# Low halves of the weights: a subtraction on VectorE replaced by an accumulating transfer from DRAM

## The chip, the cores and the metric

The kernel runs on one core of one Trainium2 chip. The metric is the device time of one execution in microseconds. Two runs of the kernel before gave 2388.38 and 2389.43 us; their median is 2388.9 us. All inputs and outputs are in DRAM (HBM) at the start and the end.

## The reference

The reference is one inference step of a two-layer trunk for 128 prompt tokens and 512 sample tokens, model width 2048, in float32. The two groups share all weights. Each layer does, for every token:

```python
h = rms_norm(x, norm_g) * (1 + scale) + shift        # scale, shift, gate = silu(cond) @ ada_w + ada_b
p = h @ w_in                                         # 2048 x 6656, all branches in one projection
y = concatenate([branch_1(p) * silu(gate_1), branch_2(p) * silu(gate_2)])
x = x + gate * (y @ w_out)                           # 2048 x 2048
```

Layer 0 has windowed grouped-query attention with a sink and a gated width-3 convolution as its branches. Layer 1 has differential attention (two softmax maps a head) and dense grouped-query attention. Sample tokens also read 256 cached keys and values and use rotary positions. The outputs are the tokens of both groups and the prompt's new keys and values.

Nearly all the arithmetic is in the projections: 640 tokens times 2 x (2048 x 6656 + 2048 x 2048) weights.

## The kernel before

**Numbers in two halves.** TensorE multiplies in a rounded form of float32 (F32R in the code). To keep float32 accuracy, each operand x is split into a high half, x rounded, and a low half, x minus the high half. A product is three matmuls: high by high, activation low by weight high, activation high by weight low.

**Blocks and quarters.** A projection job computes 128 output columns for all 640 tokens; its sum over 2048 input features runs in four quarters of 512 features. A quarter needs one weight block of 512 x 128 numbers (256 KB in DRAM, in rows of 512 bytes), held in SBUF as 128 partitions x 4 x 128. `load_raw` loads it with one transfer on SyncE's queue. `split_w` makes the halves `wh` and `wl` by the helper `split`: ScalarE rounds, VectorE subtracts. `proj_q` then runs 24 matmuls of 128 x 320: four 128-feature pieces, three products, two halves of the tokens (`pa` and `pb`). The tiles `raw`, `wh` and `wl` have four buffers each (`W_BUFS`).

**What runs ahead.** `run_tiles` runs one list of jobs: the input projection of layer 0 (52 jobs), its output projection (16), then the same for layer 1. In steady running it loads a block five quarters ahead of use (`RAW_AHEAD`) and splits it three quarters ahead (`SPLIT_AHEAD`). The first three or five jobs of a list (the leading products) run side by side, quarter by quarter, while the activations `hi` and `lo` of the layer are made. At the very start these share time with the modulation matmuls (`ada_on_pe`, tiles `ada_w`), whose weights are loaded by SyncE in blocks of 512 KB.

**What runs between quarters.** Work that follows a projection (norms, rotary, attention, gates) is cut into steps that are issued between quarters. The rest of the modulation is done on VectorE from 256 KB tiles `adaw` (`ada_on_dve`), some steps per quarter. Softmax exponentials and the rounding of attention operands run on ScalarE, the maxima, scalings and subtractions on VectorE. GpSimd computes a few small powers for the norms (tiles `r`, `rq`, `rn`) and issues the stores: finished branch outputs `y` to a scratch `yd`, the residual `x` to `xd`, the new keys and values, and the outputs. Each engine works through its own queue in order and waits at an instruction until its inputs are there and its buffer is free.

The page's line 208 is the rounding on ScalarE and line 209 the subtraction on VectorE, both in `split`, which is called for weights and for activations alike; the tile's name tells them apart. Lines 240 to 242 are the three products.

Of the kernel before, what the change touches and what calls it, by code (L numbers as in the profile page):

```python
# [15 lines left out]
ALU = mybir.AluOpType  # L16
# [4 lines left out]
P = 128  # L21
# [34 lines left out]
def trunk_kernel(ctx: ExitStack, tc: tile.TileContext, I: dict, O: dict):  # L56
# [26 lines left out]

# [1 line left out]
    ident = const.tile([P, P], F32, name="ident")  # L85
# [17 lines left out]
    for i, n in enumerate(("a_q_norm", "c_q_norm", "d_q_norm")):  # L103
        nc.scalar.dma_start(rows_b[74 + i:75 + i, :], I[n])
    # twice silu(cond) in rows, then features on partitions
    th = pre.tile([32, P], F32, name="th")
# [18 lines left out]

# [1 line left out]
    def ada_done(l, cb, h=0, n=4):  # L127
# [17 lines left out]
    def ada_on_pe(l, cb, pool, h=0, n=4):  # L145
        """The whole block, or half h of it (n of its four 128-column parts)."""
        acc, m, wd = psT(), 8 // n, n * P
        for kt in range(KT):
            if kt % m == 0:
                w = pool.tile([P, m, wd], F32, tag="ada", name="ada_w", bufs=ADA_BUFS)  # L150
                nc.sync.dma_start(w, I["ada_w"][l, kt * P:(kt + m) * P, cb * 512 + h * 256:cb * 512 + h * 256 + wd]
                                  .rearrange("(k p) n -> p k n", p=P))
            g = kt % 4
            PE.matmul(acc[32 * g:32 * g + 32, 0:wd], sT[:, kt, :], w[:, kt % m, :],  # L154
                      start=(kt < 4), stop=(kt >= KT - 4), tile_position=(0, 32 * g))
        sb = pool.tile([P, 512], F32, tag="ada_sb", name="ada_sb", bufs=1)
        A.copy(sb[:, 0:wd], acc[:, 0:wd])
        tr = psT()
        for j in range(n):
            PE.transpose(tr[:, j * P:(j + 1) * P], sb[:, j * P:(j + 1) * P], ident)  # L160
        red = small.tile([P, n, 2], F32, tag="red", name="red", bufs=2)
        V.tensor_reduce(red, tr[:, 0:wd].rearrange("p (b g c) -> p b c g", b=n, g=4)[:, :, 0:2, :], axis=AX.X,
                        op=ALU.add)
        add_bias(l, cb, red, h, n)
        ada_done(l, cb, h, n)
# [39 lines left out]

# [1 line left out]
    def split(hi, lo, x):  # L207
# [9 lines left out]

# [1 line left out]
    def load_raw(w_ap, col, qd, js=(0, 4)):  # L219
        raw = wpool.tile([P, js[1] - js[0], P], F32, tag="raw", name="raw")  # L220
        nc.sync.dma_start(raw, w_ap[(qd * 4 + js[0]) * P:(qd * 4 + js[1]) * P, col:col + P]
                          .rearrange("(k p) n -> p k n", p=P))
        return raw

    def split_w(raw):
        wh = wpool.tile(raw.shape, F32R, tag="wh", name="wh")
        wl = wpool.tile(raw.shape, F32R, tag="wl", name="wl")
        split(wh, wl, raw)
        return wh, wl
# [14 lines left out]
    def new_pp(i):  # L244
        """Two banks for a projection: a pair of them turn about, the third is the scores'."""
        if i == 2:
            t = pS.tile([P, 1024], F32, tag="S", name="Sp")
            return t[:, 0:512], t[:, 512:1024]
        return tuple(pproj.tile([P, 512], F32, tag=f"p{h}{i}", name=f"p{h}") for h in "ab")

    # Work that follows a projection runs in steps between the quarters of later projections.
    prep, attn = [], []
# [20 lines left out]
    def run_tiles(jobs, w_ap, make_h, fill=None, rate=0.0, ahead=None, order=(0, 1, 2, 3), before=None,  # L273
                  last=None, by_half=False, trans=[], grace=0, cut=None):
        if trans:
            lp = tc.tile_pool(name="lead", bufs=1, side="right")
            lead_pool = lp.__enter__()
            sums = {n: lead_pool.tile([P, NT], F32, name=f"sum{n}") for n in trans}
            held = [n for n in range(2 + len(trans)) if n not in trans]
            # a product that is summed on chip between two that stay in PSUM  # L280
            leads = [n for m in range(len(held) + 1) for n in trans[m:m + 1] + held[m:m + 1]]
            leads += trans[len(held) + 1:]
        else:
            leads, held, lp = list(range(min(3, len(jobs)))), [], None
# [4 lines left out]
        for ui, (pos, qd, js) in enumerate(units):  # L289
            parts = {n: split_w(load_raw(w_ap, jobs[n][0], qd, js)) for n in leads[:W_BUFS]}  # L290
            for hv in [HV[:1], HV[1:]] if by_half and pos == 0 else [HV]:
# [4 lines left out]
                for n in leads:  # L296
# [12 lines left out]
                    advance(attn, 1)  # L309
        # quarters of the other projections: loaded RAW_AHEAD and split SPLIT_AHEAD quarters before their use  # L310
        quarters = [(col, qd) for col, _ in jobs[lead:] for qd in range(4)]
# [17 lines left out]
        def settle():  # L329
            """Finish the work that follows the leading products."""  # L330
            while pending:
                n = pending.pop(0)
                drain(prep)
                if before:
                    before(n)
                begin(jobs[n][1], pps[n])
            drain(prep)
# [43 lines left out]
    def to_rows(src, sample):  # L381
        """Tokens on partitions: the sample's four blocks, or the prompt's one."""
        t = psT()
        for i, b in enumerate(range(4) if sample else (4,)):
            PE.transpose(t[:, i * P:(i + 1) * P], src(b), ident)  # L385
        return t if sample else t[:, 0:P]
# [10 lines left out]

# [1 line left out]
    def k_gen(ap, pp, tag, src, gain, new_out):  # L399
# [44 lines left out]

# [1 line left out]
    def q_gen(ap, pp, tag, gain, then=None, wait=True):  # L446
# [22 lines left out]
        for j in range(2):  # L469
            PE.transpose(t[:, j * 96:(j + 1) * 96], sb[:, j * P:(j + 1) * P], ident[0:96, 0:96])  # L470
        # columns: blocks 0, 2, 3 and 1, 3, 4
        u = small.tile([P, 6], F32, tag="ss", name="u")
# [36 lines left out]

# [1 line left out]
    def soft(ap, width, s, n, rsc, nsink=None, sink=None):  # L511
# [17 lines left out]
    def pt_group(ap, pieces):  # L529
        """Up to four 128-wide blocks of P, transposed and split."""  # L530
        t = psT()
        n = len(pieces) * P
        for i, p in enumerate(pieces):
            PE.transpose(t[:, i * P:(i + 1) * P], p, ident)  # L534
        hi = ap.tile([P, 512], F32R, tag="pth", name="pth", bufs=2)
        lo = ap.tile([P, 512], F32R, tag="ptl", name="ptl", bufs=2)
        split(hi[:, 0:n], lo[:, 0:n], t[:, 0:n])
        return hi, lo
# [13 lines left out]

    # the prompt's 128 keys are read with the 128 before them, which the softmax leaves out
    PROMPT_SEGS = [(0, CTX + NS - P, 2 * P)]
    DENSE_SEGS = [(128, 0, 384), (512, 384, 384)]

    def blk_plan(blk, banded):
        """Score segments, masks, the softmax's columns and the key chunks of a query block."""
        if blk == 4:
            return PROMPT_SEGS, (), P, 2 * P, [6]  # L560
        if not banded:
            return DENSE_SEGS, (), 128, 896, [0, 1, 2, 3, 4, 5]
        lo_b, hi_b = max(0, blk - 1), min(3, blk + 1)
        nb = (hi_b - lo_b + 1) * P
        masks = []
        if blk > 0:
            masks.append((mask_lo, 512))
        if blk < 3:
            masks.append((mask_hi, 512 + (blk + 1 - lo_b) * P))
        return ([(256, 0, CTX), (512, CTX + lo_b * P, nb)], masks, 256, 512 + nb,  # L570
                [0, 1] + [2 + b for b in range(lo_b, hi_b + 1)])

    def pair_gen(ap, width, k, banded, emit, done, sinks):
        """Two query heads that share keys and values."""
        v = st["v"]
# [93 lines left out]

    # ======== start: x normalised and transposed, layer 0 modulation ========  # L670
    xT = [sp.tile([P, 4, NT], F32, name=f"xT{g}") for g in range(4)]
# [57 lines left out]

    # ======== layer 0: windowed attention and gated short convolution ========  # L730
    def k_job(tag, src, gain, new_out):
# [13 lines left out]
    def pair_then(width, kk, i, banded, gated):  # L745
        """Attention of heads whose outputs are y[i] and y[i + 1]."""
        def then():
# [88 lines left out]
    for _ in fill0:  # L836
        pass
    # output projection, residual
    x1 = [None] * KT
# [46 lines left out]

    # layer 1 normalisation: half of the tokens while the last product of the other half runs
    def out_last(pp, h):
# [47 lines left out]

    # ======== layer 1: differential attention and dense attention ========
    def odd_start():
# [24 lines left out]
    def diff_gen(ap, h, gt):  # L963
        """Two softmax maps over the same values, the second weighted by -lambda."""
        v = st["v"]
# [166 lines left out]
def _shape_constants():  # L1132
    """Arrays that depend on shapes alone: identity, rotary tables, band edges."""
    t = np.arange(NS)
# [34 lines left out]
```

## Time and profile before

| | |
|---|---|
| median of two runs | 2388.9 us |
| span of the profiled execution (no other time is recorded for it) | 2390.2 us |
| TensorE busy | 2349.4 us, 98% |
| VectorE busy | 1368.3 us, 57% |
| ScalarE busy | 882.6 us, 37% |
| GpSimd busy | 122.9 us, 5% |
| bytes moved by transfers | 298.86 MB, mean 125 GB/s |
| share of the 16 DMA engines, hardware and software queues | 38.1% and 2.7% |

PE is TensorE, ACT is ScalarE, DVE is VectorE, POOL is GpSimd and SP is SyncE; a "q" behind the name is the engine's queue for transfers. The hardware queue carries what SyncE and ScalarE issue, the software queue what GpSimd issues. A group of instructions is shown as line, engine, operation, output and inputs, shape and count, then busy time and mean duration in ns, then the idle time before it and what ended that. Matmuls overlap in the pipeline, so their durations add up to more than the span. "DMA share" is the mean busy share of the 16 DMA engines in a stretch.

### The profile page before, as it was taken

What the parts mean: (1) busy time and instruction counts of PE and PEld (TensorE: products, weight loads), DVE (VectorE), ACT (ScalarE), POOL (GpSimd) and SP (SyncE); (2) the same over time, 40 slices, a digit from 0 to 9 for tenths busy, and PEclk for the clock granted to TensorE, in tenths of its full rate; (3) what the DMA queues carried; (4) which work ended last, traced back from release to release, by engine and by line L of the source; (5) the groups of instructions that cost most, each with busy time, mean ns of one, the idle gap of its engine ahead of it and who ended that gap; (6) DMA issues with size and microseconds to landing.
All of it is one profiled execution on the core that took longest, in us unless ns stands there. A gap on an engine that the chain in (4) does not pass through costs nothing.

```text
span 2390.2 us, 41198 instructions
## 1 busy us (share of the span) xinstructions
PE 2349.4 (98%) x16258; PEld 2252.1 (94%) x16258; DVE 1368.3 (57%) x2711; ACT 882.6 (37%) x1878; POOL 122.9 (5%) x169
## 2 busy tenths in 40 slices
PE   6999999999999999999999999999999999999999
PEld 3579999999999999999999999999999999999999
DVE  4268666765855564666775535454454554576562
ACT  4135342443421223222374434434434444453221
POOL 0001000000000000000000100101000000000000
PEclk9999999999999999999999999999999999999999
DMA  9774325424444445666532221212222212236552
GB/s 330 249 241 132 115 80 157 140 62 150 125 146 126 137 135 158 195 180 191 147 95 65 72 77 54 84 56 83 66 73 59 65 49 80 61 115 213 186 171 79
DMA packets 380128, 298.86 MB, mean 125 GB/s; under 512 B 17842, under 2 KB 321519, under 8 KB 379935
## 3 DMA queue, kind: packets, MB, share of 16 engines
q1 hardware_dynamic: 373104, 273.79, 38.1%
q0 software_dynamic: 6288, 22.22, 2.7%
q8 instruction: 128, 2.10, 0.4%
q14 instruction: 66, 0.53, 0.1%
q10 hardware_dynamic: 542, 0.22, 0.0%
HBM read 273.62 MB, written 22.54 MB: 124 GB/s over the span
## 4 chain that ended last, share of the span: by engine, by line
PE 91%; DVE 3%; DMA 3%; ACT 2%; issue 1%; POOL 0%; SPq 0%; DVEq 0%; ACTq 0%; POOLq 0%
PE pa L240 12%; PE pb L241 12%; PE pb L240 12%; PE pb L242 12%; PE pa L242 12%; PE pa L241 12%; PE T L534 2%; PE T L154 2%; PE S L546 1%; PE S L548 1%; PE S L547 1%; PE T L385 1%; PE T L595 1%; DVE acc L180 1%; DMA ada_w<-in_ada_w 1%
## 5 line engine op out<-in xcount | busy, mean ns | idle before, releaser
L208 ACT ACTIVATE wh<-raw 128x512 fp32r<-128x512 f32 (+1 forms) x549 | 342.9, 627 | 1026.1 <-PE pb L241 895.3
L209 DVE TENSOR_TENSOR wl<-raw,wh 128x512 fp32r<-128x512 f32 (+1 forms) x549 | 374.7, 684 | 534.7 <-ACT wh L208 487.3
L240 PE MATMUL pa<-hi,wh 128*128 128x320 f32 x2112 | 671.9, 318 | 4.7 <-DVE gg L777 1.7
L241 PE MATMUL pa<-lo,wh 128*128 128x320 f32 x2112 | 655.6, 311 | 1.0 <-DVE lo L209 1.0
L242 PE MATMUL pa<-hi,wl 128*128 128x320 f32 x2112 | 654.3, 310 | 0.3 <-DVE wl L209 0.3
L242 PE MATMUL pb<-hi,wl 128*128 128x320 f32 x2112 | 654.2, 310 | 0.0
L240 PE MATMUL pb<-hi,wh 128*128 128x320 f32 x2112 | 653.5, 310 | 0.0
L241 PE MATMUL pb<-lo,wh 128*128 128x320 f32 x2112 | 653.5, 309 | 0.0
L240 PEld LDWEIGHTS pa<-hi,wh 128*128 128x128 f32 x2112 | 397.5, 188 | 28.5 <-issue 20.2
L241 PEld LDWEIGHTS pa<-lo,wh 128*128 128x128 f32 x2112 | 398.1, 189 | 4.9 <-issue 2.9
L241 PEld LDWEIGHTS pb<-lo,wh 128*128 128x128 f32 x2112 | 396.6, 188 | 3.8 <-issue 3.8
L242 PEld LDWEIGHTS pb<-hi,wl 128*128 128x128 f32 x2112 | 396.6, 188 | 3.8 <-issue 3.8
L240 PEld LDWEIGHTS pb<-hi,wh 128*128 128x128 f32 x2112 | 396.5, 188 | 3.3 <-issue 3.3
L242 PEld LDWEIGHTS pa<-hi,wl 128*128 128x128 f32 x2112 | 397.3, 188 | 2.1 <-issue 1.2
L180 DVE SCALAR_TENSOR_TENSOR acc<-adaw,sT,acc 128x512 f32<-128x512 f32 x480 | 336.4, 744 | 27.7 <-DMA adaw<-in_ada_w 27.2
L520 ACT ACTIVATE p<-S,nm,rq 128x768 f32<-128x768 f32 (+3 forms) x120 | 101.2, 844 | 116.8 <-DVE nm L515 80.8
L513 DVE TENSOR_REDUCE nm<-S 128x1 f32<-128x768 f32 (+3 forms) x120 | 91.8, 765 | 23.3 <-PE S L548 22.8
L208 ACT ACTIVATE pth<-T 128x512 fp32r<-128x512 f32 (+1 forms) x132 | 65.7, 533 | 64.6 <-PE T L534 64.5
L209 DVE TENSOR_TENSOR ptl<-T,pth 128x512 fp32r<-128x512 f32 (+1 forms) x132 | 77.3, 608 | 6.2 <-ACT pth L208 4.8
L534 PE MATMUL T<-ident,p 128*128 128x128 f32 x452 | 64.5, 273 | 0.1
L454 ACT COPY qsw<-qx 32x512 f32<-32x512 f32 x96 | 59.3, 618 | 5.6 <-DVE m L430 4.2
L154 PE MATMUL T<-ada_w,sT 128*32 128x512 f32 (+1 forms) x320 | 54.1, 530 | 3.7 <-DMA ada_w<-in_ada_w 3.3
(247 smaller groups left out, 2302.0 us busy)
## 6 DMA issues: line engine op xcount, KB each, us to landing
adaw<-in_ada_w SPq DMA_DIRECT2D x256, 256.0 KB, 3.2
raw<-in_od_w_in SPq DMA_DIRECT2D x208, 256.0 KB, 2.9
raw<-in_ev_w_in SPq DMA_DIRECT2D x203, 256.0 KB, 3.0
ada_w<-in_ada_w SPq DMA_DIRECT2D x64, 512.0 KB, 7.2
raw<-in_ev_w_out SPq DMA_DIRECT2D x64, 256.0 KB, 2.9
raw<-in_od_w_out SPq DMA_DIRECT2D x64, 256.0 KB, 2.9
yd<-y POOLq DMA_DIRECT2D x32, 320.0 KB, 3.0
yin<-yd SPq DMA_DIRECT2D x28, 320.0 KB, 4.1
```

The lines of the kernel that those rows point to most:

```text
L154: PE.matmul(acc[32 * g:32 * g + 32, 0:wd], sT[:, kt, :], w[:, kt % m, :], start=(kt < 4), stop=(kt >= KT - 4), tile_position=(0, 32 * g))
L180: V.scalar_tensor_tensor(out=acc[c], in0=w, scalar=sT[:, kt, c:c + 1], in1=acc[c], op0=ALU.mult, op1=ALU.add)
L208: A.activation(hi, x, AF.Copy)
L209: V.tensor_sub(lo, x, hi)
L240: PE.matmul(ps, wh[:, i, :], hi[:, sl], start=(j == js[0] if alone else (pos == 0 and j == 0)), stop=False)
L241: PE.matmul(ps, wh[:, i, :], lo[:, sl], start=False, stop=False)
L242: PE.matmul(ps, wl[:, i, :], hi[:, sl], start=False, stop=(j == js[1] - 1 if alone else (pos == 3 and j == 3)))
L385: PE.transpose(t[:, i * P:(i + 1) * P], src(b), ident)
L454: A.copy(sw[32 * d:32 * d + 32, :], x[32 * (d ^ 1):32 * (d ^ 1) + 32, 0:NS])
L513: V.tensor_reduce(nm, s, axis=AX.X, op=ALU.max, negate=True)
L520: A.activation(p[:, 0:n], s, AF.Exp, scale=rsc, bias=nm, accum_out=l)
L534: PE.transpose(t[:, i * P:(i + 1) * P], p, ident)
```

## The change

The low half of a weight block is made in another way. ScalarE writes minus the rounded block into `wl`. A transfer issued by GpSimd then reads the same block from DRAM a second time and adds it to what `wl` holds, so that `wl` becomes the block minus its rounded form. ScalarE then writes `wh` as before. VectorE takes no part. `load_raw` returns the DRAM view beside the tile, so that `split_w` can name it. The splitting of activations (`split`) is as before. The lines of comments that the diff also drops are left out here.

```diff
     def load_raw(w_ap, col, qd, js=(0, 4)):
         raw = wpool.tile([P, js[1] - js[0], P], F32, tag="raw", name="raw")
-        nc.sync.dma_start(raw, w_ap[(qd * 4 + js[0]) * P:(qd * 4 + js[1]) * P, col:col + P]
-                          .rearrange("(k p) n -> p k n", p=P))
-        return raw
+        src = w_ap[(qd * 4 + js[0]) * P:(qd * 4 + js[1]) * P, col:col + P].rearrange("(k p) n -> p k n", p=P)
+        nc.sync.dma_start(raw, src)
+        return raw, src
 
     def split_w(raw):
+        raw, src = raw
         wh = wpool.tile(raw.shape, F32R, tag="wh", name="wh")
         wl = wpool.tile(raw.shape, F32R, tag="wl", name="wl")
-        split(wh, wl, raw)
+        A.activation(wl, raw, AF.Copy, scale=-1.0)
+        nc.gpsimd.dma_start(wl, src, accum_op=ALU.add)
+        A.activation(wh, raw, AF.Copy)
         return wh, wl
```

## The prediction

> **What bounds the kernel now.** I read the page's totals first, then the chain that ended last, then its groups.
>
> ```profile
> span 2390.2 us, 41198 instructions
> ...
> PE 2349.4 (98%) x16258; PEld 2252.1 (94%) x16258; DVE 1368.3 (57%) x2711; ACT 882.6 (37%) x1878; POOL 122.9 (5%) x169
> ...
> q1 hardware_dynamic: 373104, 273.79, 38.1%
> q0 software_dynamic: 6288, 22.22, 2.7%
> ...
> PE 91%; DVE 3%; DMA 3%; ACT 2%; issue 1%; POOL 0%; SPq 0%; DVEq 0%; ACTq 0%; POOLq 0%
> ...
> L208 ACT ACTIVATE wh<-raw 128x512 fp32r<-128x512 f32 (+1 forms) x549 | 342.9, 627 | 1026.1 <-PE pb L241 895.3
> L209 DVE TENSOR_TENSOR wl<-raw,wh 128x512 fp32r<-128x512 f32 (+1 forms) x549 | 374.7, 684 | 534.7 <-ACT wh L208 487.3
> ```
>
> TensorE is busy for 98% of the span and makes 91% of the chain. VectorE, which the change relieves, has 57%, and its subtraction (684 ns, 549 times) mostly waits for ScalarE. TensorE idles 2390.2 - 2349.4 = 41 us in all, so no edit that leaves the matmuls alone gains more than that, 1.7%. How far ahead of use is a block made? The timeline of the first output projection shows the third product's matmuls on the low half, and the two halves being made:
>
> ```profile
> 1061.73 0.69 DVE L209 TENSOR_TENSOR wl<-raw,wh 128x512 fp32r<-128x512 f32 x1
> ...
> 1062.27 0.31 PE L242 MATMUL pb<-hi,wl 128*128 128x320 f32 x1
> ...
> 1062.47 0.63 ACT L208 ACTIVATE wh<-raw 128x512 fp32r<-128x512 f32 x1 [2.84 <-PE pb L241]
> ...
> 1065.37 0.68 DVE L209 TENSOR_TENSOR wl<-raw,wh 128x512 fp32r<-128x512 f32 x1
> ...
> 1065.79 0.31 PE L242 MATMUL pb<-hi,wl 128*128 128x320 f32 x1
> ```
>
> From the last matmul of one quarter (1062.27) to that of the next (1065.79) is 3.52 us. ScalarE starts at 1062.47, when a quarter has just released a buffer. There are four buffers, so that one is next read after the other three, 3 x 3.52 = 10.6 us later. Today the low half is ready at 1066.05, 3.8 us after the release. The other resource the change uses is the transfers, so I cut the span into stages; the matmuls of line 242 count the blocks used (eight a block):
>
> ```profile
> core 0: us, PE busy (x) PEld busy (x), PEclk, DMA share, GB/s
> 0.00:60.00 60.00, 1.94 (x6) 1.13 (x6) 0.97 0.95 330
> 60.00:180.00 120.00, 49.77 (x160) 30.02 (x161) 1.00 0.75 245
> 180.00:480.00 300.00, 173.51 (x561) 105.31 (x561) 1.00 0.42 125
> 480.00:900.00 420.00, 264.49 (x855) 160.40 (x855) 1.00 0.42 126
> 900.00:960.00 60.00, 40.48 (x131) 24.65 (x132) 1.00 0.55 169
> 960.00:1140.00 180.00, 116.50 (x376) 70.98 (x376) 0.99 0.63 186
> 1140.00:1320.00 180.00, 104.57 (x338) 63.33 (x337) 1.00 0.34 99
> 1320.00:2100.00 780.00, 422.66 (x1368) 256.74 (x1367) 1.00 0.23 69
> 2100.00:2160.00 60.00, 23.66 (x77) 14.46 (x77) 1.00 0.43 142
> 2160.00:2340.00 180.00, 119.80 (x388) 72.69 (x387) 1.00 0.59 181
> 2340.00:2390.00 50.00, 29.75 (x96) 18.02 (x96) 1.00 0.23 67
> ```
>
> The mean share hides this: the DMA engines are 75% busy in the first products, 63% and 59% in the two output projections, and 23% in the long attention stage.
>
> **The change part by part.**
>
> *Compute engines.* VectorE loses 549 subtractions, 374.7 us. ScalarE gains 549 passes over the same block; priced as its own rounding (627 ns) that is 344 us, and it goes from 37% to 51%. GpSimd gains 549 issues. Its transfers today, and what transfers take to land:
>
> ```profile
> L656 POOL DMA_DIRECT2D yd<-y x32 | 17.9, 561 | 752.2 <-DVE y L779 532.4 <-DVE y L753 125.8 <-DMA adaw<-in_ada_w 43.9
> L1096 POOL DMA_DIRECT2D out_y_sample<-ot x15 | 11.4, 758 | 206.9 <-ACT ot L1095 206.9
> ```
>
> ```profile
> raw<-in_od_w_in SPq DMA_DIRECT2D x208, 256.0 KB, 2.9
> ...
> out_y_sample<-ot POOLq DMA_DIRECT2D x15, 256.0 KB, 3.9
> xb<-in_x_prompt SPq DMA_DIRECT2D x4, 256.0 KB, 6.4
> ```
>
> The nearest issue is out_y_sample: 256 KB, DRAM rows of 512 bytes as in a weight block, 758 ns. 549 x 0.758 = 416 us more on an engine that is busy 5%. No row shows an accumulating issue; I take 0.76 and bound it by 0.56 (yd, longer rows) and by two such issues, 1.5. None of the three engines becomes full.
>
> *Latency of a low half.* After the release: about 0.2 us, ScalarE 0.63, about 0.1, GpSimd 0.76, then the landing. At the plain landing of 3.9 the sum is 5.6 us, against 3.8 now and 10.6 allowed: 5 us of cover are left. That cover is gone when a landing takes more than 10.6 - 1.7 = 8.9 us; the slowest median of a 256 KB transfer, from the start where the share is 0.95, is 6.4. So I cost the latency in steady running at nothing.
>
> *Queues it is put into.* GpSimd's queue is in order, and the added issue waits for ScalarE. Behind it stand the powers of the norms (r, rq, rn) and the stores of y, x and the outputs. The nearest is rn:
>
> ```profile
> DVE on L1009 <- POOL rn L1008: 14.5, 20, 0.8
> ```
>
> An issue ahead of it makes it up to 0.76 us later, 20 times; the next reader on TensorE is a quarter of matmuls (3.52 us) behind, so nothing. The other way round, a store that waits for VectorE holds the next block's issue for some 2 or 3 us, inside the 5 us of cover. On ScalarE exponentials and rounding of attention stand 0.63 us later behind the extra pass, and VectorE's half of the same chain is 0.68 us earlier: nothing. SP issues the same loads; a raw buffer is now free after ScalarE's second pass instead of VectorE's, 0.63 for 0.68: nothing.
>
> *Transfer time.* This is the term that counts. The change adds 549 blocks, 143 MB beside 299. A block by the hardware queue's rate costs all engines 0.381 x 2390.2 / 273.79 x 0.262 = 0.87 us; by the software queue's, 0.027 x 2390.2 / 22.22 x 0.262 = 0.76. The trace has no accumulating transfer. From below it costs one plain software transfer, 0.76. It must also fetch what the block holds in SBUF, so the nearest rows are a load from DRAM (0.87) plus a transfer that reads SBUF (0.76): 1.63, the value I take. From above I set three copies (two reads and a write, each as a load): 2.6.
>
> By stage, at 1.63: 60 to 180 us has 160/8 = 20 blocks, 20 x 1.63 / 120 = 0.27, share 1.02; 900 to 960 has 16.4, share 0.55 + 0.45 = 1.00; 960 to 1140 has 47, 0.63 + 0.43 = 1.06; 2160 to 2340 has 48.5, 0.59 + 0.44 = 1.03. All others stay under 0.85 (480 to 900: 0.42 + 0.42). What exceeds 1 lengthens the stage: 0.02 x 120 + 0.06 x 180 + 0.03 x 180 = 18 us. At 0.76 no stage exceeds 0.88 and the term is 0.
>
> The Trainium skill (Collectives: The Full Stack, Part 3, "The bandwidth ceiling") says that an add in the transfer engines needs two source reads on one ring and so runs at about half a copy's rate, measured at a ratio of 1.93. By that page, as an estimate, a block would cost 1.93 x 0.87 = 1.7 us and the term would be about 27 us in place of 18. No run here shows it yet.
>
> *Start.* Two places are not covered by running ahead.
>
> ```profile
> 40.00:70.00 30.00, 25.32 (x137) 11.46 (x136) 10.47 (x23) 8.19 (x14) 0.00 (x0) 1.00 1.00 349
> 70.00:90.00 20.00, 19.10 (x102) 11.45 (x102) 3.36 (x9) 3.95 (x8) 0.00 (x0) 1.00 0.35 109
> ```
>
> ```profile
> 50.31 1.20 DVE wl L209 x2
> ...
> 124.67 4.28 DMA raw<-in_ev_w_in
> ...
> 129.05 0.64 ACT wh L208
> ...
> 129.74 0.41 PE Sp L240
> ```
>
> From 40 to 70 us the transfers are full; the first four blocks add 4 x 1.63 = 6.5 us there, and the idle transfers from 70 to 90 (0.35) give most of it back: 2 us. At 124.67 the chain itself runs through a raw block to the matmul; its low half would land 0.63 + 0.76 + 3.9 = 5.3 us after it instead of 1.3: 4 us. Against this, subtractions leave the chain ahead of the first product (50.31): -1 us.
>
> Sum: 18 + 2 + 4 - 1 = 23 us; 2390.2 + 23 = 2413. The span stands 1.3 us above the runs' median of 2388.9, and no other time of the profiled execution is recorded, so I predict **2412 us**, +1%. A change of 2% (48 us; faster than 2341 or slower than 2437) is about what a measurement of this kernel can tell from no change.
>
> **The rivals.**
>
> *Hidden.* A block costs a plain copy (0.76). No stage fills; left are the start's few us: 2386 to 2395. For it: the mean share would be 41% + 549 x 0.76 / 2390 = 58%. Against it: the second read.
>
> *Slower: the transfers become the bound.* The place is the first products, the windowed stage and both output projections, the price is the block's transfer time. It decides from about 1.9 us a block, where the surplus of the four stages passes 48 us with the start. At 2.6: 60 to 180, 1.18, 22 us; 180 to 480 (70 blocks), 1.03, 8; 480 to 900 (107), 1.08, 35; 900 to 960, 1.26, 16; 960 to 1140, 1.31, 56; 2160 to 2340, 1.29, 52: 189 us, 2579. Landing time adds to it: once L, the time from release to landed, exceeds 10.6, the quarter becomes (L + 3.52) / 4, so 2 us more is 0.5 us in each of the 110 or so quarters of the output projections: 55 us. For it: three stages are at the brim already at 1.63. Against it: the long attention stage has room at any of these prices (0.23 + 0.57).
>
> *Slower: GpSimd's issue is the bound.* If an accumulating issue takes more than 3.52 us, the projections go at its pace; at 6 us, 549 x 6 = 3290. Nothing in the trace shows an issue over 0.77 us, and nothing shows one of this kind.
>
> *Faster by over 2%.* It would need 48 us where TensorE idles 41. That the subtraction isn't gone is excluded: the built order has none on VectorE, and 549 more passes on ScalarE and transfers on GpSimd.
>
> **How the numbers follow.** Forecast, 2395 to 2437: 0.38. Hidden: 0.12. Transfers the bound, 2437 to about 2600: 0.36. GpSimd's issue or a landing beyond all rows, above 2600: 0.13. Faster: 0.01. So within 2% is 0.50, slower 0.49, faster 0.01. The range reaches from 2388, inside the hidden case, to 2600, the price of 2.6 with a little landing on top; it leaves out the issue's case and the lowest part of the hidden one. The forecast's own range is 2395 to 2437.
>
> **What would show it.** Right: ScalarE near 1227 us and VectorE near 994; the software queue at 37% of the engines (2.7% + 549 x 1.63 / 2390) and the share at or near 1 in the output projections, 0.6 in the attention stage; landing of the added transfers 4 to 7 us; TensorE's waits for them short, and most of them in those full stages. Hidden: software queue near 20%. Wrong: an added issue that lasts microseconds on GpSimd, a landing above 9 us, or TensorE waiting for low halves in the attention stage too.

## The result, and the profile after

The changed kernel takes 2519.74 us (median of 2517.21 and 2522.26) where the kernel before takes 2388.9: a ratio of 1.0545, 95% interval 1.0528 to 1.0563. The profiled execution has a span of 2520.5 us, 130.3 us longer than before's. The page's totals, its queues and the chain that ended last:

```profile
span 2520.5 us, 42146 instructions
...
PE 2391.6 (95%) x16258; PEld 2285.0 (91%) x16258; DVE 1050.4 (42%) x2162; ACT 1153.2 (46%) x2427; POOL 833.7 (33%) x718
...
q0 software_dynamic: 293600, 164.86, 48.7%
q1 hardware_dynamic: 373104, 273.79, 36.2%
...
PE 73%; DMA 12%; issue 8%; DVE 4%; POOL 1%; ACT 1%; SPq 0%; POOLq 0%; ACTq 0%; DVEq 0%
```

VectorE has lost 318 us of work, and no compute engine but TensorE is near full. TensorE runs the same 16258 matmuls, but idles 2520.5 - 2391.6 = 128.9 us (40.8 before) and is busy 42.2 us longer. 88.1 + 42.2 = 130.3: both need a cause. Transfers are now 12% of the chain (3% before). The page's groups, then its DMA issues (last column: median us from issue to landing):

```profile
L245 PE MATMUL pa<-hi,wl 128*128 128x320 f32 x2112 | 667.2, 316 | 60.5 <-DMA wl<-in_ev_w_in 34.0
...
L230 POOL DMA_DIRECT2D wl<-in_ev_w_in x213 | 274.0, 1349 | 597.6 <-ACT wl L229 463.6
...
L180 DVE SCALAR_TENSOR_TENSOR acc<-adaw,sT,acc 128x512 f32<-128x512 f32 x480 | 339.2, 748 | 143.1 <-DMA adaw<-in_ada_w 141.6
L229 ACT ACTIVATE wl<-raw 128x512 fp32r<-128x512 f32 (+1 forms) x549 | 336.0, 615 | 14.8 <-PE pb L245 14.2
...
wl<-in_od_w_in POOLq DMA_DIRECT2D x208, 256.0 KB, 5.3
...
wl<-in_ev_w_in POOLq DMA_DIRECT2D x203, 256.0 KB, 6.0
...
wl<-in_ev_w_out POOLq DMA_DIRECT2D x64, 256.0 KB, 6.5
```

The same two groups before:

```profile
L242 PE MATMUL pa<-hi,wl 128*128 128x320 f32 x2112 | 654.3, 310 | 0.3 <-DVE wl L209 0.3
...
L180 DVE SCALAR_TENSOR_TENSOR acc<-adaw,sT,acc 128x512 f32<-128x512 f32 x480 | 336.4, 744 | 27.7 <-DMA adaw<-in_ada_w 27.2
```

An issue of an added transfer holds GpSimd for 1.3 us, and its landing takes 5.3 to 6.5 us by the medians of the groups. The third product (line 245, line 242 before) now waits 60.5 us where it waited 0.3, and most of that is for the added transfers. VectorE waits 141.6 us for modulation tiles `adaw`, 27.2 before. TensorE's waits, as total us, times and longest:

```profile
PE pa L245 <- DMA wl<-in_ev_w_in: 34.0, 13, 8.2
PE pa L245 <- DMA wl<-in_ev_w_out: 15.4, 5, 5.4
...
PE pa L245 <- DMA wl<-in_od_w_in: 7.7, 5, 3.4
```

**Where the time goes.** The 549 blocks are used in the same order in every kernel here, so the start of each block's third product can be set against the same one of before. The table gives this lag in us at the edges of the stages; a stage's loss is the difference of two neighbours. Here and below the lags are those of the profiled executions.

| third product of | before, at us | lag after |
|---|---|---|
| block 0 | 54.0 | 4.2 |
| block 32 (start is over) | 232.4 | 45.0 |
| block 208 (first output projection begins) | 939.0 | 64.1 |
| block 272 (turn to layer 1) | 1185.3 | 101.8 |
| block 304 | 1326.5 | 117.4 |
| block 480 (last output projection begins) | 2147.7 | 117.5 |
| end | 2390.2 | 130.3 |

So the start loses 45 us, the rest of layer 0's input projection 19, the first output projection 38, the turn to layer 1 16, the long attention stage nothing, the last projection 13. The windows of the same stages (columns after the stretch and its length: busy time of PE, PEld, DVE, ACT and POOL, the granted clock, the DMA share, GB/s):

```profile
60.00:200.00 140.00, 116.35 (x689) 76.50 (x687) 32.29 (x79) 31.73 (x65) 24.00 (x19) 0.91 0.85 225
1003.00:1079.00 76.00, 65.48 (x408) 64.33 (x408) 35.11 (x55) 28.48 (x53) 22.85 (x20) 0.87 1.07 244
1137.00:1280.00 143.00, 125.58 (x816) 122.58 (x814) 67.17 (x116) 44.62 (x86) 42.91 (x38) 0.92 0.99 214
1420.00:2200.00 780.00, 778.20 (x5447) 764.49 (x5447) 291.34 (x649) 417.50 (x914) 270.93 (x237) 1.00 0.70 123
```

At a share of 0.70 nothing is lost. Where TensorE falls behind in these windows, the share is about 1 or the activations and weights are being made at the last moment (the start), and the granted clock is low too: 0.87 to 0.92. Shares above 1 occur, so 1 is no ceiling of this measure.

**The clock.** Two neighbouring windows around one wait of TensorE show why it is also busy for longer:

```profile
1155.29:1162.12 6.83, 4.04 (x15) 4.05 (x16) 0.15 (x1) 0.00 (x0) 1.40 (x2) 0.50 1.30 217
1162.12:1166.00 3.88, 3.88 (x30) 3.88 (x29) 0.00 (x0) 1.79 (x4) 1.24 (x1) 1.00 1.23 253
```

In the first, TensorE idles 2.8 us and runs 15 matmuls in 4.04 us, 0.27 each, at clock 0.50; in the second 30 in 3.88, 0.13 each, at 1.00. Within the span the clock stands at 0.5 for 116.1 us in 20 stretches, before for 6.8 us in 2. In them TensorE is busy for 87.5 us (6.4 before); at full clock the same work would take half, so they explain (87.5 - 6.4) / 2 = 40.5 of the 42.2 us. A shorter wait can do it too:

```profile
1322.60:1326.00 3.40, 1.48 (x10) 1.20 (x9) 3.37 (x7) 3.40 (x8) 0.74 (x1) 0.99 1.14 182
1326.00:1329.40 3.40, 3.40 (x15) 3.40 (x14) 2.10 (x5) 1.63 (x4) 0.54 (x1) 0.50 0.61 105
```

In the first row TensorE idles 1.92 us of the 3.4, and the whole of the second runs at half clock. The Trainium skill (TensorE: Matmul & The Clock Gate, Part 1) says that the clock halves after an idle window of about 3.4 us and recovers after as long a busy one. The stretches here last 3.4, 6.8, 10.2 and once 13.7 us, which fits windows of that length; but the two rows show the halving behind a window that was idle for little more than half of it, and there the measurement decides.

**Two chains.** At the start, the timelines of ScalarE and GpSimd and then the chain that ended last:

```profile
91.24 0.58 ACT L157 COPY ada_sb<-T 128x512 f32<-128x512 f32 x1 [7.66 <-PE T L154]
91.72 0.63 ACT L229 ACTIVATE wl<-raw 128x512 fp32r<-128x512 f32 x1
...
92.64 5.23 POOL L230 DMA_DIRECT2D wl<-in_ev_w_in  x4 [39.17 <-PE T L160]
```

```profile
92.64 9.26 DMA wl<-in_ev_w_in
...
101.95 0.63 PE pa L245
```

ScalarE's queue stands at a modulation copy for 7.66 us; the four blocks behind it are then made in one go, their issues take 5.23 us, and the landing 9.26 us, with TensorE at the end of it. In the first output projection the same happens by another road (VectorE, ScalarE, GpSimd, then the chain):

```profile
1212.47 2.74 DVE L180 SCALAR_TENSOR_TENSOR acc<-adaw,sT,acc 128x512 f32<-128x512 f32 x4 [4.36 <-DMA adaw<-in_ada_w]
1215.12 0.55 DVE L873 SCALAR_TENSOR_TENSOR x<-pa,hgt,o 128x320 f32<-128x320 f32 x1
...
1216.29 0.74 ACT L886 ACTIVATE sq<-x 128x640 f32<-128x640 f32 x1 [10.48 <-DVE x L873]
...
1216.55 0.59 POOL L881 DMA_DIRECT2D xd<-x  x1 [11.93 <-DVE x L873]
1217.13 2.63 POOL L230 DMA_DIRECT2D wl<-in_ev_w_out  x2
```

```profile
1217.13 8.20 DMA wl<-in_ev_w_out
...
1225.37 0.64 PE pa L245
```

A late modulation tile `adaw` holds VectorE, so the residual `x` is late; ScalarE's square and GpSimd's store of `x` wait for it 10.5 and 11.9 us, and the next low halves stand behind both. The traces alone don't tell how much of this is the transfers' bandwidth and how much the lateness of the low half in itself. That is what the runs are for.

### The profile page after: what moved, and what is told of

Same layout as the page of the kernel before. It is cut to its first block, busy times and chain, and to the rows that moved or that the text cites. A ratio compares the mean times of both kernels' runs of the same rounds, so it can differ in the third digit from the quotient of the medians.

```text
span 2520.5 us, 42146 instructions
## 1 busy us (share of the span) xinstructions
PE 2391.6 (95%) x16258; PEld 2285.0 (91%) x16258; DVE 1050.4 (42%) x2162; ACT 1153.2 (46%) x2427; POOL 833.7 (33%) x718
## 3 DMA queue, kind: packets, MB, share of 16 engines
q0 software_dynamic: 293600, 164.86, 48.7%
## 4 chain that ended last, share of the span: by engine, by line
PE 73%; DMA 12%; issue 8%; DVE 4%; POOL 1%; ACT 1%; SPq 0%; POOLq 0%; ACTq 0%; DVEq 0%
PE pa L245 10%; PE pa L243 10%; PE pb L244 10%; PE pb L243 10%; PE pb L245 10%; PE pa L244 10%; DMA adaw<-in_ada_w 4%; DMA wl<-in_ev_w_in 3%; PE T L537 2%; DVE acc L180 2%; DMA ada_w<-in_ada_w 2%; PE S L549 1%; PE S L551 1%; PE S L550 1%; PE T L388 1%
## 5 line engine op out<-in xcount | busy, mean ns | idle before, releaser
L245 PE MATMUL pa<-hi,wl 128*128 128x320 f32 x2112 | 667.2, 316 | 60.5 <-DMA wl<-in_ev_w_in 34.0
L243 PE MATMUL pb<-hi,wh 128*128 128x320 f32 x2112 | 660.2, 313 | 0.0
L230 POOL DMA_DIRECT2D wl<-in_ev_w_in x213 | 274.0, 1349 | 597.6 <-ACT wl L229 463.6
L245 PEld LDWEIGHTS pa<-hi,wl 128*128 128x128 f32 x2112 | 404.1, 191 | 71.8 <-DMA wl<-in_ev_w_in 37.5
L230 POOL DMA_DIRECT2D wl<-in_od_w_in x208 | 270.0, 1331 | 528.8 <-ACT wl L229 433.8
L243 PEld LDWEIGHTS pb<-hi,wh 128*128 128x128 f32 x2112 | 403.0, 191 | 3.4 <-issue 3.4
L180 DVE SCALAR_TENSOR_TENSOR acc<-adaw,sT,acc 128x512 f32<-128x512 f32 x480 | 339.2, 748 | 143.1 <-DMA adaw<-in_ada_w 141.6
L229 ACT ACTIVATE wl<-raw 128x512 fp32r<-128x512 f32 (+1 forms) x549 | 336.0, 615 | 14.8 <-PE pb L245 14.2
L230 POOL DMA_DIRECT2D wl<-in_od_w_out x64 | 82.9, 1295 | 166.8 <-ACT wl L229 159.6
L230 POOL DMA_DIRECT2D wl<-in_ev_w_out x64 | 83.0, 1312 | 128.6 <-ACT wl L229 122.9
```

What stands on the lines that cost most here:

```text
L180: V.scalar_tensor_tensor(out=acc[c], in0=w, scalar=sT[:, kt, c:c + 1], in1=acc[c], op0=ALU.mult, op1=ALU.add)
L229: A.activation(wl, raw, AF.Copy, scale=-1.0)
L230: nc.gpsimd.dma_start(wl, src, accum_op=ALU.add)
L243: PE.matmul(ps, wh[:, i, :], hi[:, sl], start=(j == js[0] if alone else (pos == 0 and j == 0)), stop=False)
L245: PE.matmul(ps, wl[:, i, :], hi[:, sl], start=False, stop=(j == js[1] - 1 if alone else (pos == 3 and j == 3)))
```

## The experiments

Theory A: the transfers. A block costs the transfer engines more than the 1.63 us that I took; where the share is already high everything lands late. Theory B: lateness. A low half now passes ScalarE, GpSimd's queue, an issue and a landing, and where blocks are made just before use, or where one of these queues is held, TensorE waits for it, even with transfers to spare. Theory C: the compute engines' added passes. The lags of all runs at the table's edges, which the text below uses:

| kernel | block 0 | 32 | 208 | 272 | 304 | 480 | end |
|---|---|---|---|---|---|---|---|
| after | 4.2 | 45.0 | 64.1 | 101.8 | 117.4 | 117.5 | 130.3 |
| e1_no_transfer | 0.6 | 1.8 | 3.0 | 5.4 | 6.7 | 4.3 | 4.7 |
| e2_plain_copy | 2.1 | 22.9 | 26.4 | 37.2 | 41.1 | 38.7 | 44.3 |
| e3_side_traffic | 0 | 34.7 | 99.5 | 148.0 | 154.2 | 156.7 | 194.7 |
| e10_plain_copy_same_type | -0.3 | 12.2 | 16.5 | 34.9 | 34.5 | 35.5 | 55.2 |
| e5_traffic_to_dram | 1.0 | 26.2 | 28.8 | 58.5 | 58.7 | 59.9 | 75.7 |
| e4_leading_subtracted | -0.6 | 7.9 | 22.4 | 51.4 | 52.1 | 51.8 | 62.0 |
| e8_only_steady_inputs | -0.4 | 10.6 | 27.8 | 25.1 | 25.7 | 25.3 | 26.1 |
| e9_powers_without_wait | 0.6 | 7.7 | 19.4 | 18.0 | 16.4 | 15.6 | 17.4 |
| e6_few_modulation_loads | 4.4 | 45.9 | 65.3 | 71.8 | 84.5 | 84.8 | 103.9 |
| e7_squares_on_vector | 2.8 | 43.8 | 63.3 | 94.2 | 106.8 | 106.5 | 120.7 |

### Without the added transfer

```diff
         A.activation(wl, raw, AF.Copy, scale=-1.0)
-        nc.gpsimd.dma_start(wl, src, accum_op=ALU.add)
         A.activation(wh, raw, AF.Copy)
```

> The change without its transfer: ScalarE makes both passes, nothing is added from DRAM (the low half stays minus the rounded block; that part of the computation is left out). Theory A (the added transfers fill the DMA engines where the share was already 0.6 to 0.75, and what waits for other loads then holds the queues): the 130 us are gone, 2385 to 2400. Theory B (the low half comes too late because of the longer chain release - ScalarE - GpSimd - landing, whatever the load on the engines): also 2385 to 2400, since the chain ends on ScalarE. A rival, ScalarE's second pass in front of the attention's rounding and exponentials: 2420 or more.

Measured: 2393.07 us, ratio 1.0003 (0.9993 to 1.0014). The page's engines:

```profile
span 2394.9 us, 40976 instructions
...
PE 2350.7 (98%) x16258; PEld 2253.6 (94%) x16258; DVE 1042.6 (44%) x2162; ACT 1156.0 (48%) x2427; POOL 123.7 (5%) x169
```

Theory C falls: ScalarE's 549 passes and VectorE's 549 missing subtractions change nothing. The whole loss hangs on the transfer. It also shows that the change had nothing to win: even a low half that costs no transfer at all gains no time, since the subtraction was hidden.

### A plain copy in place of the addition

```diff
-        nc.gpsimd.dma_start(wl, src, accum_op=ALU.add)
+        nc.gpsimd.dma_start(wl, src)
```

> The added transfer copies the block instead of adding it (the low half then holds the whole block; the subtraction is left out). Same number of transfers, same issues and waits, no second read. Theory A: a plain copy costs about 0.8 us of all engines instead of 2.1, the output projections stay at a share of 0.85, and most of the loss goes: 2390 to 2425. Theory B: issue and landing are hardly shorter (1.0 to 1.3 and 4 to 5 us), the leading products still wait: 2440 to 2510.

Measured: 2438.74 us, 1.0200 (1.0183 to 1.0217). The issues' group and the window of the long attention stage:

```profile
L230 POOL DMA_DIRECT2D wl<-in_ev_w_in x213 | 159.1, 747 | 682.8 <-ACT wl L229 539.6 <-PE T L160 71.8 <-ACT wh L231 14.6
```

```profile
1360.00:2140.00 780.00, 779.15 (x5457) 765.57 (x5456) 287.24 (x638) 421.42 (x918) 182.66 (x241) 1.00 0.55 126
```

The order of the queues is as in the changed kernel, but an issue takes 0.75 us and the share is 0.55. A block's price follows from the share in this stage less before's 0.23, times 780 us over the stage's 171 blocks: 0.32 x 780 / 171 = 1.46 us here, 0.47 x 780 / 171 = 2.14 in the changed kernel (each to some 0.05, by the share's rounding). With the cheaper transfer two thirds of the loss are gone. The time lies in neither theory's range, and since issue, landing and price all fell together, this run alone doesn't part A from B. It does show that lateness is not a fixed cost of the longer road: on the same road the turn to layer 1 loses 4 us instead of 16.

### The accumulation as mere traffic, into the raw block

Before's kernel, which subtracts on VectorE; behind the split the same transfer adds to the raw tile, which nothing reads any more.

```diff
         split(wh, wl, raw)
+        nc.gpsimd.dma_start(raw, src, accum_op=ALU.add)
```

> The kernel before, with its subtraction on VectorE, plus the same 549 accumulating transfers into the raw tile once it has been split, where no matmul reads them. The traffic of the change without its latency. Theory A: most of the loss is there: 2450 to 2510, with the output projections at a share of 1. Theory B: 2390 to 2420.

Measured: 2594.03 us, 1.0851 (1.0814 to 1.0887), slower than the change itself and outside both ranges. One of ScalarE's waits, and the long attention stage:

```profile
ACT wh L208 <- DMA raw<-in_ev_w_in: 211.6, 64, 9.3
```

```profile
1500.00:2280.00 780.00, 778.87 (x5434) 763.25 (x5433) 393.25 (x811) 337.28 (x741) 273.85 (x238) 1.00 0.71 126
```

The run doesn't test what it was made for: the transfer holds the raw buffer until it has landed, so the next load is late, and ScalarE waits 211.6 us for raw blocks. What it does give is the price with a float32 destination: 0.48 x 780 / 171 = 2.19 us, the same as with the rounded type.

The same with a plain copy (a single run, no interval):

```diff
-        nc.gpsimd.dma_start(raw, src, accum_op=ALU.add)
+        nc.gpsimd.dma_start(raw, src)
```

> For the price of a block alone: the third experiment with a plain copy into the raw tile, float32 to float32, in place of the addition. In the long attention stage the copy of the second experiment cost 1.46 us of all engines a block and the hardware queue's load of the same rows 0.87. If the conversion to the rounded type makes the difference: about 0.9. If it is the software queue's small packets: about 1.4 to 1.5.

Measured: 2447.16 us. Its software queue and the same stage:

```profile
q0 software_dynamic: 49888, 164.86, 21.1%
```

```profile
1400.00:2180.00 780.00, 779.03 (x5439) 763.48 (x5438) 398.84 (x826) 334.72 (x730) 176.89 (x230) 1.00 0.41 124
```

0.18 x 780 / 171 = 0.82 us a block, my lower bound of 0.76 nearly. With the plain copy between equal types the software queue carries its bytes in 49888 packets; with the addition, and likewise with the copy that converts (e2_plain_copy), in 293600. The small packets by themselves are not the price, though: the trace of before has the hardware queue's loads of the same rows in packets of 512 bytes too, 28 ns each on average. Such a packet takes 43 ns in the converting copy and 66 ns in the addition, with (the changed kernel) or without (e3_side_traffic) a conversion.

### The accumulation as mere traffic, into DRAM

Before's kernel; each low half is also added into one of eight scratch tiles in DRAM (the first eight copied). No later work reads these tiles, but the transfer reads `wl`, whose buffer isn't free until then.

```diff
         split(wh, wl, raw)
+        i = turn[0]
+        turn[0] += 1
+        if i < 8:
+            nc.gpsimd.dma_start(side[i][:, 0:raw.shape[1], 0:P], wl)
+        else:
+            nc.gpsimd.dma_start(side[i % 8][:, 0:raw.shape[1], 0:P], wl, accum_op=ALU.add)
```

> The kernel before, with its subtraction on VectorE, plus 549 accumulating transfers that nothing waits for: each adds the finished low half to a scratch in DRAM, in rows of 512 bytes (two reads and a write, as in the change, the write to DRAM). In the third experiment the raw buffers were held by the transfers, so loads came late too; here only the traffic and the issues are added. Theory A (the traffic itself, in full stages): 2440 to 2520, the first output projection and the start behind as in the change. Theory B (the late low half): within 15 us of before, 2390 to 2405, though the engines' share is as high as in the change.

Measured: 2465.68 us, 1.0315 (1.0299 to 1.0330). Windows:

```profile
480.00:900.00 420.00, 419.95 (x2949) 412.56 (x2948) 274.03 (x531) 130.95 (x271) 135.80 (x118) 1.00 1.03 196
...
960.00:1140.00 180.00, 164.61 (x1116) 161.85 (x1116) 102.97 (x172) 49.80 (x90) 58.73 (x55) 0.95 1.13 236
```

```profile
1380.00:2160.00 780.00, 778.91 (x5442) 763.81 (x5441) 387.49 (x806) 334.31 (x743) 258.09 (x240) 1.00 0.79 126
```

The low half that TensorE reads is VectorE's and waits for no transfer to land; traffic and issues still cost 75 us. By the table: 26 to block 32, 30 in the first output projection, 16 in the last, and 3, 0 and 1 elsewhere. Two caveats. Into DRAM a block costs 0.56 x 780 / 171 = 2.55 us, somewhat more than the change's 2.14. And some lateness is left, from `wl` buffers that a transfer still holds:

```profile
DVE wl L209 <- DMA side<-wl: 15.7, 6, 4.5
...
PE pa L251 <- DVE wl L209: 7.7, 7, 3.9
```

Four of the six waits, and 5.8 of the 7.7 us, fall in the first output projection. So theory A is shown for the greater part of the output projections' loss and for some of the start. It doesn't explain layer 0's steady projection (3 here, 19 after) nor the turn to layer 1 (0 here, 16 after). The stretch behind block 272 in the changed kernel and then in this one shows the turn:

```profile
1287.00:1330.00 43.00, 35.69 (x195) 33.65 (x195) 22.99 (x52) 27.34 (x58) 10.50 (x9) 0.80 0.64 111
```

```profile
1243.00:1290.00 47.00, 46.78 (x326) 45.88 (x325) 35.07 (x75) 34.07 (x72) 15.74 (x14) 1.00 0.96 166
```

The change loses time there at a share of 0.64, this run almost none at 0.96. The first of the earlier windows also holds a surprise: 420 us at a share of 1.03 in which TensorE is never idle.

### Leading products subtracted on VectorE

```diff
-            parts = {n: split_w(load_raw(w_ap, jobs[n][0], qd, js)) for n in leads[:W_BUFS]}
+            parts = {n: split_w(load_raw(w_ap, jobs[n][0], qd, js), True) for n in leads[:W_BUFS]}
```

`split_w(raw, True)` uses the old `split`; so does the second call in the leading products.

> The change, but the blocks of the leading products (the first three or five jobs of each of the four lists, about 66 of 549 blocks) are subtracted on VectorE as before; all others come by the accumulating transfer. Theory A: the first output projection keeps its loss and the start gets back only what about 24 transfers less are worth there: 2470 to 2500. Theory B: the start (45 us behind by the 32nd block) and the turn to layer 1 (some 30 us) come back: 2430 to 2450.

Measured: 2454.16 us, 1.0250 (1.0229 to 1.0271), 4 us above theory B's range: half of the loss hangs on the blocks of the leading products, some 11% of all. The start loses 8 instead of 45 and the turn to layer 1 1 instead of 16, while the first output projection still loses 29. In the turn e5_traffic_to_dram, with the traffic and without the lateness, lost nothing either; so it is lateness there (theory B). At the start the edit takes away 37 us, of which traffic by itself can be 26, if the two simply add up; the other 11 or more are then lateness.

### Output projections subtracted too

On top of the last edit:

```diff
-                    parts[j] = split_w(raws[j])
+                    parts[j] = split_w(raws[j], before is not None or last is not None)
```

> The change in the steady part of the two input projections alone; the leading products and both output projections subtract on VectorE. 395 or so of 549 blocks still come by transfer, in stages where the share was 0.94 and 0.72. Both theories: no full stage and no leading product is left, 2395 to 2420 (the fourth experiment was 22 us behind at block 208, all of it in layer 0). If a long attention stage with transfers at 0.7 cost something after all, 2430 or more.

Measured: 2418.78 us, 1.0117 (1.0100 to 1.0134). The first output projection's loss is gone (25.1 - 27.8, none), and the last one's. What is left is in layer 0's input projection, 17 us between blocks 32 and 208, and it isn't bandwidth: e5_traffic_to_dram lost 3 there. The timelines of ScalarE and GpSimd before one of TensorE's waits (317.7 to 322.9):

```profile
312.44 0.61 ACT L232 ACTIVATE wl<-raw 128x512 fp32r<-128x512 f32 x1
...
314.36 1.72 POOL L483 TENSOR_TENSOR rq<-u,half 128x6 f32<-128x6 f32 x1 [8.97 <-DVE u L479]
316.04 2.64 POOL L233 DMA_DIRECT2D wl<-in_ev_w_in  x2
```

The block's first pass is done at 313.05, but GpSimd stands for 8.97 us at the power `rq`, which waits for VectorE, and issues at 316.04.

### The powers without their wait

On top of it, the powers on GpSimd take a constant in place of VectorE's result (the norms' scales are thus not those of the data):

```diff
-        G.tensor_tensor(r, ss, half[:, 0:5], op=ALU.pow)
+        G.tensor_tensor(r, ones[:, 0:5], half[:, 0:5], op=ALU.pow)
...
-        G.tensor_tensor(r6, u, half[:, 0:6], op=ALU.pow)
+        G.tensor_tensor(r6, ones[:, 0:6], half[:, 0:6], op=ALU.pow)
```

> The eighth experiment (2419 us, 26 us behind, 17 of them in layer 0 between blocks 32 and 208), with the powers of the query and key norms on GpSimd taken from a constant instead of from VectorE's sums (the norms of queries and keys are left out), so that GpSimd's queue does not wait there. Queue theory (an issue stands behind a power that waits for VectorE, seen at 305 to 316 us): 5 to 12 of the 17 us come back, 2405 to 2414. If only ScalarE's hold or the transfers' length make those low halves late: 2416 to 2421.

Measured: 2409.09 us, 1.0072 (1.0055 to 1.0089); 9.7 us less, with intervals that don't touch, about a third of what e8_only_steady_inputs loses. By the table 5.5 us of it come back between blocks 32 and 208, and most of the rest at the start. TensorE's wait of 317.7 to 322.9 (5.2 us, at block 49) is down to 1.6. So GpSimd's queue in order is shown as a cause; its exact share isn't, since the edit also spares the engines that use the powers their own wait for them. Between blocks 32 and 208 still 12 us are lost; the stores of `y` and ScalarE's own queue are left as candidates, not tried.

### Fewer modulation loads in the first output projection

The changed kernel; of each 16 tiles `adaw` of that stage only the first is loaded, and used 16 times (60 loads fewer; the modulation is thus not that of the data).

```diff
-                w = ap.tile([P, 512], F32, tag=wt[kt % 3], name="adaw", bufs=bufs)
-                nc.sync.dma_start(w, ada_src(l, cb, kt, 1).rearrange("p k n -> p (k n)"))
+                if kt == 0 or not once:
+                    w = ap.tile([P, 512], F32, tag=wt[kt % 3], name="adaw", bufs=bufs)
+                    nc.sync.dma_start(w, ada_src(l, cb, kt, 1).rearrange("p k n -> p (k n)"))
```

> The change, but in the first output projection the modulation on VectorE loads one tile in 16 and uses it 16 times (the other 60 loads of 256 KB and so the right values of four modulation blocks are left out; VectorE's work is the same). Theory A: that stage falls from a share of 1.03 to about 0.75, and its 50 us of loss (blocks 224 to 288) go but for the turn to layer 1: 2475 to 2490. Theory B: 2510 to 2522.

Measured: 2490.11 us, 1.0418 (1.0401 to 1.0435). The stage loses 6.5 us instead of 38:

```profile
1004.00:1075.00 71.00, 63.92 (x415) 62.44 (x415) 33.90 (x56) 29.27 (x54) 23.50 (x22) 0.96 1.00 209
1075.00:1190.00 115.00, 115.00 (x803) 113.66 (x802) 56.30 (x98) 45.75 (x87) 43.96 (x38) 1.00 0.97 187
```

With the low halves made exactly as in the changed kernel, and 60 loads of 0.87 us, 52 us of transfer time, taken away, TensorE is full in the stage's second part. It is a matter of too many transfers there; but the edit removes the late `adaw` at the same time, so it doesn't tell the share of that chain from the rest of the crowding.

### Squares on VectorE

The changed kernel, with ScalarE no longer waiting for `x` at line 886:

```diff
-                A.activation(sq, x1[n], AF.Square)
+                V.tensor_mul(sq, x1[n], x1[n])
```

> The change, but the squares of the new residual in the first output projection (15 of 16 products) are made on VectorE, so that ScalarE's queue, in which the passes for the weight blocks stand, no longer waits there for VectorE. Traffic is the same. Theory A: no gain, 2510 to 2525. Theory B, with ScalarE's queue held by a late residual as the reason that the low halves are late in that stage: 20 to 35 us come back, 2485 to 2500.

Measured: 2519.66 us, 1.0536 (1.0517 to 1.0554); the changed kernel has 1.0545 (1.0528 to 1.0563), so no gain. That ScalarE is held 10.5 us is no cause by itself: the store `xd` on GpSimd waits for the same `x` and is still ahead of the next issue (this is the reading of the timeline above; the store was not moved).

## Why the prediction came out as it did

The forecast was 2412 us, no change within 2%; the time is 2519.74, 130.3 us on the profiled span where the sum had 23. The time lies in the range of the rival in which transfers become the bound, 2437 to 2600, but only about half of the loss is that rival's mechanism (75 of 130 us in e5_traffic_to_dram, at a higher price a block); that its range holds the time is in part luck. Three steps of the forecast's sum failed: the price of a block, the rule that turns shares above 1 into time, and the latency and the queues taken at nothing. A fourth term, the clock, is not in it.

- **What bounds the kernel.** Right: TensorE, with nothing to win. e1_no_transfer, the change without its transfer, stands at 1.0003.
- **Compute engines at nothing.** Right, by the same run. ScalarE came to 1153 us (1227 forecast), VectorE to 1050 (994).
- **GpSimd's issue.** Taken at 0.76 us, measured at 1.3, inside its bounds of 0.56 to 1.5; the plain copy takes 0.75. GpSimd is busy 834 us and never the bound by its load.
- **Price of a block: mis-sized.** 2.14 us in place of 1.63, inside 0.76 to 2.6 and past the rival's threshold of 1.9. The two nearest rows, a load and a store, gave too little: an adding transfer takes 66 ns for a packet of 512 bytes where a load takes 28.
- **A share above 1 as the only cost, and all of it a loss: failed.** At 2.14 the prediction's sum by stage gives 13 us for 60 to 180 us, 8 for 900 to 960, 0.63 + 47 x 2.14 / 180 = 1.19 and so 34 for 960 to 1140, and 30 for 2160 to 2340. Together they are 85 us in place of 18. Transfers in full stages did cost time, but not by this rule: the last output projection loses 13 us in all, and at the 2.55 of e5_traffic_to_dram the same sum gives about 170 us where that run loses 75, with a stage at 1.03 that loses next to nothing. That the 85 lies near the 75 of that run is chance. In the stages that are full, what the traces show is loads such as `adaw` landing late and holding the queues behind them.
- **The Trainium skill's estimate** (Collectives: The Full Stack, Part 3, a ratio of 1.93 for an add, measured there between two collectives): against before's load the price is 2.14 / 0.87 = 2.5, against the plain copy of e10_plain_copy_same_type 2.14 / 0.82 = 2.6, against the converting copy of e2_plain_copy 1.47. The figure of the Trainium skill is none of these; the measurement decides.
- **Latency of a low half, costed at nothing: failed for the leading products.** The cover of 10.6 us exists in steady running alone. Where a list of jobs begins, blocks are made just before use, and I had looked at the very start only (4 us). Lateness costs about 15 us at the turn to layer 1 and, by the reckoning of e4_leading_subtracted, at least 11 of the start's 45. Single landings of the added transfers last up to 20.3 us (median 5.7), past the 8.9 that the cover allowed.
- **Queue blocking of 2 or 3 us inside 5 us of cover: failed.** GpSimd stands up to 9 us at a power (e8_only_steady_inputs) and 11.9 us at the store of `x` (the changed kernel), and the blocks behind it are issued in a burst whose landing is 8 to 9 us. Undoing the powers' wait alone gave 9.7 us back.
- **A step that the sum doesn't have: the clock.** The longer of TensorE's waits are followed by time at half clock; TensorE is busy 42 of the 130 us longer, and the half clock explains 40.5 of them.
- **What was to show it.** Software queue at 37% of the engines: 48.7% (the terms named there, 2.7% and 549 x 1.63 / 2390, add up to 40%). Share near 1 in the output projections and 0.6 in the attention stage: 1.07 and 0.70. Landing 4 to 7 us: 5.3 to 6.5 by the groups' medians, though the sign for "wrong" of a landing above 9 us did come in single ones. TensorE's waits for low halves short and mostly in the full stages: 57 us in all, up to 8.2 us each, 24 of them at the start. The sign of TensorE waiting in the attention stage didn't come: 778.2 of 780 us are busy there, as the prediction had it at any price.

By stage, then: the first and the last output projection (38 and 13 us) are mainly the transfers' traffic. Traffic at a higher price costs 30 and 16 there (e5_traffic_to_dram), 60 loads fewer give 31 of the 38 back (e6_few_modulation_loads), and without added transfers there is no loss (e8_only_steady_inputs). How much of the 38 is lateness stays open. The turn (16) and most of layer 0's steady projection (19) are lateness (e4_leading_subtracted, e5_traffic_to_dram, e9_powers_without_wait). At the start (45) both act, traffic with up to 26; how the two divide there is open, since no run had the lateness without the traffic. Nor are the two independent: a cheaper transfer is also issued and landed sooner (e2_plain_copy).

## What to carry to other kernels

Before moving a hidden operation from an engine to a transfer, ask what the operation costs where it is: with nothing to win, only the new price is left. Cost the transfer stage by stage and at a measured price for that kind: here an adding transfer cost 2.6 times a plain one and a converting one 1.8 times. And walk every queue that it passes, at the places where work is made just before use as well as in steady running. Count a wait of TensorE at more than its length where, as here, the clock drops behind it.

## What was not expected of the hardware

- A 256 KB block in rows of 512 bytes costs all transfer engines 0.82 us as a plain software copy, 1.46 with a conversion of the type, 2.14 with an addition in SBUF and 2.55 with an addition in DRAM. Addition and conversion go in packets of 512 bytes (66 and 43 ns each), the plain copy in packets of 4096; the hardware queue's loads go in packets of 512 bytes as well, at 28 ns.
- A DMA share of 1 is not by itself a limit: 420 us at 1.03 left TensorE without a gap, 180 us at 1.13 left it idle for 15 us (both e5_traffic_to_dram).
- Behind waits of 1.9 to 8.2 us the clock stood at half for stretches of 3.4 to 13.7 us; a few stretches followed several shorter waits. In all it was 116.1 us.
